# The output projection of a three-branch layer as seven block products instead of a plain tiled product

## The chip, the cores and the metric

The kernel runs on one core of one Trainium2 chip, in one launch. The metric is device time in microseconds (us). Three runs of the kernel before took 2734.89, 2730.94 and 2734.28 us, a median of 2734.28 us.

## The reference

Two layers are applied to x, a 1024 x 1024 matrix of fp32 (1024 positions, width 1024). Each layer norms x, multiplies it by w_in, runs three branches (an attention with top-k selection, a stick-breaking attention, an mLSTM), and mixes them; after both layers a last rms norm gives the output. What matters here is the end of a layer:

```
proj  = einsum('bsgc,gcd->bsgd', branches, w_branch)   # per branch 1024x512 by 512x1024
gates = sigmoid(merge)                                  # 3 x 1024 x 1024
mixed = sum over g of gates * proj                      # 1024 x 1024
x     = x + mixed @ w_out                               # 1024x1024 by 1024x1024
```

The next layer (or the end) begins with rms_norm of the rows of x.

## The kernel before

All products are done in float32r with a split: each operand is cut into a rounded part (hi, made by a ScalarE copy) and the remainder (lo, a subtraction on VectorE, or on GpSimd in pieces of 256 columns), and three passes hi·hi, hi·lo, lo·hi are summed in PSUM (`PASSES`). So each 128-deep step of a product is three matmuls.

The program is first written down as a log of operations by `body`; then the class `Plan` puts them in order. It walks through modelled time, gives each engine the ready operation that stands earliest in the log (`key`), gives each tile a buffer when its first operation is dispatched, and emits the whole in that order. Each engine then runs its own list strictly in that order. Tiles of SBUF are of two main sizes: `half` (128 x 520, `N_HALF` = 21 buffers) and `slab` (128 x 1032, `N_SLAB` = 35 buffers); a slab can also be split into two halves of the same type. `LOOK` (line 93) keeps an operation that needs a new half or slab from being taken more than 400 log entries ahead of the first one that is not done, and `room` (line 316) keeps an early tile from taking space that the log needs before it. PSUM has eight banks of 128 x 512: six of class `ps` and two of class `psf`. All DMAs are issued by the SP queue, in the plan's order.

The end of a layer (from line 1578): the gates were computed earlier and stored to DRAM (`gate_d`). For branches 2 and 1 (loop at line 1612) `load_y` brings the branch's hi and lo tiles, and for each of eight column blocks d and two row halves th `gate_proj` loads the gate and does 12 matmuls of 512 columns; VectorE multiplies, GpSimd adds into `mixed[d][th]`. For branch 0 the loop over th is outside: for each half of the rows, 8 x 12 matmuls, then VectorE adds and the sum is cut into hi and lo; then the output projection of this half: for each pair of column blocks cp two `load_w` of w_out (each 8 k-tiles: two DMAs of 512 KB, two ScalarE copies, eight GpSimd subtractions), and for four row tiles t two groups of 24 matmuls of 256 columns, after which VectorE adds the PSUM tile to the x row. So w_out and branch 0's weights are loaded and cut twice in a layer. Then the four rows are stored (`x_nd`, layer 0 only), normed in place (`norm_rows`: ScalarE square with sum, a small VectorE op, a power on GpSimd, a VectorE multiply `scalar_tensor_tensor` that writes the row back over itself), and `transpose_h` turns them with 32 TensorE transposes for the next layer; in the last layer the normed rows go to the output.

Of the kernel before, what the change touches and what calls it, by code (L numbers as in the profile page):

```python
# [11 lines left out]
F32R = mybir.dt.float32r  # L12
# [3 lines left out]
ALU = mybir.AluOpType  # L16
# [4 lines left out]
T = 1024  # L21
D = 1024
NB = 8
DEPTH = 2
# [9 lines left out]
PASSES = ((0, 0), (0, 1), (1, 0))  # L34
# [579 lines left out]
def body(log, tiles, caps, x_in, w_in, w_uk, w_uv, kvn, conv_w, ib, fb, mln, w_br, w_out, nrm, fnrm,  # L614
         rope_t, out, stop=None, dbg=None):
    V, S, G, PE, SY = (Engine(log, e) for e in ("DVE", "ACT", "POOL", "PE", "SP"))
# [6 lines left out]
    def slab(dt=F32):  # L623
        return tiles.new("slab", [128, 1032], dt)

    def half(dt=F32, n=520):
        return tiles.new("half", [128, n], dt)

    def pair(dt=F32):
        t = slab(dt)  # L630
        return t[:, 0:512], t[:, 512:1024]
# [8 lines left out]
    def pst(tag, n=512):  # L640
        return tiles.new(tag if tag == "psf" else "ps", [128, 512], F32)

    def dram(shape, dt=F32):
        return tiles.new("dram", shape, dt)
# [27 lines left out]
    for j in range(8):  # L672
        k = (j % 4) + 8 * (j // 4)
# [18 lines left out]
    def pool_tt(dst, a, b, op, n, w=256):  # L692
        for c in range(0, n, w):
            e = min(n, c + w)
            G.tensor_tensor(dst[:, c:e], a[:, c:e], b[:, c:e], op)

    def split(src, hi, lo, n=None):
        S.copy(hi, src)
        if n:
            pool_tt(lo, src, f(hi), ALU.subtract, n)  # L700
        else:
            V.tensor_tensor(lo, src, f(hi), ALU.subtract)

    def load_w(pieces, nk=8):
        W = [[], []]
        n = max(o + a.shape[1] for a, o in pieces)
        for hb in range(nk // 4):
            def view(t):
                return t[:, :1024].rearrange("p (k c) -> p k c", k=4)[:, :, :n]
            st, wh, wl = slab(), slab(F32R), slab(F32R)  # L710
            for a, o in pieces:
                m = a.shape[1]
                SY.dma_start(view(st)[:, :, o:o + m],
                             a[hb * 512:(hb + 1) * 512, :].rearrange("(k p) c -> p k c", p=128))
            S.copy(view(wh), view(st))
            for k in range(4):
                G.tensor_tensor(view(wl)[:, k], view(st)[:, k], f(view(wh)[:, k]), ALU.subtract)
            W[0].append(wh)
            W[1].append(wl)
        return W  # L720
# [13 lines left out]
    def acc_tc(p, W, n, sta, nk=8):  # L734
        i = 0
        for a, b in PASSES:
            for k in range(nk):
                PE.matmul(p[:, :n], sta(b, k), wcol(W, a, k, 0, n), start=(i == 0), stop=(i == 3 * nk - 1))
                i += 1
# [8 lines left out]
    def norm_rows(x, nw, dst):  # L748
        ss = small([128, 4], name="ss", bufs=8)
        junk = half(BF16, 1040)  # L750
        S.activation(junk[:, :1024], x[:, :1024], AF.Square, accum_out=ss[:, 0:1])
        V.tensor_scalar(ss[:, 1:2], ss[:, 0:1], 1.0 / D, EPS, ALU.mult, ALU.add)
        rsqrt(ss[:, 2:3], ss[:, 1:2])
        V.scalar_tensor_tensor(dst[:, :1024], x[:, :1024], ss[:, 2:3], nw[:, :1024], ALU.mult, ALU.mult)

    def transpose_h(hn, hT, th):
        for kb in range(8):
            p = pst("tr")
            for t in range(4):
                PE.transpose(p[:, t * 128:t * 128 + 128], hn[t][:, kb * 128:kb * 128 + 128], ident)  # L760
            hi, lo = pair(F32R)
            split(p, hi, lo)
            hT[0][kb][th], hT[1][kb][th] = hi, lo

    def new_hT():
        return [[[None, None] for _ in range(8)] for _ in range(2)]

    def load_row(vec):
        w = slab()
        SY.dma_start(w[:, :1024], bcast(vec, 1024))  # L770
        return w
# [9 lines left out]
    for th in range(2):  # L781
        hn = []
        for t in range(4):
            tb = th * 4 + t
            x = slab()
# [10 lines left out]
    x_res = x_in[0]  # L796
    for l in range(DEPTH):
# [25 lines left out]
        for tb in range(2, 8):  # L823
            if tb % 2 == 0:
                iq.append(half())
            p = pst("mm")
# [3 lines left out]
        for tb in range(8):  # L830
            if tb % 2 == 0:
                pb.append(half())
            p = pst("mm")
# [35 lines left out]
        for th in range(2):  # L869
            p = pst("tr")  # L870
# [7 lines left out]
        for tb in range(2, 8):  # L878
# [5 lines left out]
            p = pst("tr")  # L884
# [697 lines left out]
        def load_y(g, ths):  # L1582
            for b in range(4):
                for a in range(2):
                    if len(ths) == 2 and b < 2:
                        t = slab(F32R)
                        ym[b, a] = (t[:, 0:512], t[:, 512:1024])
                    else:
                        ym[b, a] = [half(F32R)[:, :512] if th in ths else None for th in range(2)]
                    for th in ths:  # L1590
                        SY.dma_start(f(ym[b, a][th]), f(y_d[g][a][b][:, th * 512:th * 512 + 512]))
# [4 lines left out]
        def gate_proj(Wm, Wp, j, th, kept=None):  # L1596
            g = half()
            if kept is None:
                p = pst("mm")
                acc_ct(p, Wm, j, mov, th)  # L1600
                S.activation(g[:, :512], p, AF.Sigmoid)
            else:
                SY.dma_start(g[:, :512], kept)
            p = pst("lg")
            acc_ct(p, Wp, j, ymov, th, nk=4)
            return g, p

        def wm(g, ct):
            return (None if g in AHEAD else load_w([(cols(C_MERGE + g * 1024 + ct * 256, 256), 0)]),
                    load_w([(w_br[l, g][:, ct * 256:ct * 256 + 256], 0)], nk=4))  # L1610

        for gi, g in enumerate((2, 1)):
            load_y(g, (0, 1))
            for ct in range(4):
                Wm, Wp = wm(g, ct)
                for j in range(2):
                    for th in range(2):
                        d = 2 * ct + j
                        gt_, p = gate_proj(Wm, Wp, j, th, gate_d.get((g, d, th)))
                        if gi == 0:  # L1620
                            mixed[d][th] = gt_
                            V.tensor_tensor(gt_[:, :512], gt_[:, :512], p, ALU.mult)
                        else:
                            V.tensor_tensor(gt_[:, :512], gt_[:, :512], p, ALU.mult)
                            pool_tt(mixed[d][th], mixed[d][th], gt_, ALU.add, 512)
        last = l == DEPTH - 1
        hT_n = new_hT()
        x_nd = None if last else dram([T, D])
        nwn = load_row(fnrm if last else nrm[l + 1])
        for th in range(2):  # L1630
            load_y(0, (th,))
            mx = [[None] * 8, [None] * 8]
            for ct in range(4):
                Wm, Wp = wm(0, ct)
                for j in range(2):
                    d = 2 * ct + j
                    gt_, p = gate_proj(Wm, Wp, j, th, gate_d.get((0, d, th)))
                    m = mixed[d][th]
                    V.tensor_tensor(gt_[:, :512], gt_[:, :512], p, ALU.mult)
                    V.tensor_tensor(m[:, :512], m[:, :512], gt_[:, :512], ALU.add)  # L1640
                    mx[0][d], mx[1][d] = hi, lo = pair(F32R)
                    split(m[:, :512], hi, lo)
            xs = []
            for cp in range(2):
                Wo = [load_w([(w_out[l][:, (2 * cp + i) * 256:(2 * cp + i) * 256 + 256], 0)]) for i in range(2)]
                for t in range(4):
                    tb = th * 4 + t
                    if cp == 0:
                        x = slab()
                        SY.dma_start(x[:, :1024], x_res[tb * 128:tb * 128 + 128, :])  # L1650
                        xs.append(x)
                    p = pst("mm")
                    for i in range(2):
                        acc_tc(p[:, 256 * i:256 * i + 256], Wo[i], 256,
                               lambda b, k: mx[b][k][:, t * 128:t * 128 + 128])
                    xx = xs[t][:, cp * 512:cp * 512 + 512]
                    V.tensor_tensor(xx, p, xx, ALU.add)
            hn = []
            for t in range(4):
                tb = th * 4 + t  # L1660
                if not last:
                    SY.dma_start(x_nd[tb * 128:tb * 128 + 128, :], xs[t][:, :1024])
                norm_rows(xs[t], nwn, xs[t])
                hn.append(xs[t])
                if last:
                    SY.dma_start(out[0, tb * 128:tb * 128 + 128, :], xs[t][:, :1024])
            if not last:
                transpose_h(hn, hT_n, th)
        hT = hT_n
        x_res = x_nd  # L1670
        if stop == "l0":
# [33 lines left out]
```

## Time and profile before

| | us |
|---|---|
| median of 3 runs | 2734.28 |
| the profiled execution | 2734.7 |
| its span, first to last instruction | 2732.9 |
| TensorE matmul busy | 2690.6 (98%) |
| VectorE busy | 1670.8 (61%) |
| ScalarE busy | 1474.7 (54%) |
| GpSimd busy | 1109.0 (41%) |
| mean granted TensorE clock | 0.996 of full speed |

Busy time is the time in which an engine had an instruction under way. PE is TensorE, PEld its weight loads (beside the matmuls), DVE is VectorE, ACT ScalarE, POOL GpSimd, SP the queue that issues DMAs. Since nearly every operation is emitted by one helper line (533), lines don't tell operations apart: shapes, engines and moments do. In layer 0 the end of the layer runs from about 1097 to 1382 us, in layer 1 from about 2500 us to the end.

### The profile page before, as it was taken

The numbers are of one execution on the slowest core, as the hardware profiler recorded it, in microseconds if no ns is written. First come the engines' busy times: TensorE is split into PE (matmuls) and PEld (weight loads), VectorE is DVE, ScalarE is ACT, GpSimd is POOL, SyncE is SP. The second block draws the span as 40 slices with busy tenths as digits, with TensorE's granted clock in tenths as the row PEclk, the third lists the DMA queues.
The fourth block names the chain that finished last, engine by engine and source line by source line (L and its number), as shares of the span: only waits on it lengthen the run. The fifth ranks groups of instructions, "written<-read, shape, count | busy, mean of one in ns | idle before, by whom it ended". The sixth has DMA issues, their size and how long they took to land.

```text
span 2732.9 us, 43639 instructions
## 1 busy us (share of the span) xinstructions
PE 2690.6 (98%) x15658; PEld 2306.7 (84%) x15666; DVE 1670.8 (61%) x3964; ACT 1474.7 (54%) x2961; POOL 1109.0 (41%) x1481
## 2 busy tenths in 40 slices
PE   8999999999999999999899999999999999999998
PEld 7888878888888888889898888888888888888898
DVE  5828788666686663424447287896676776624244
ACT  4637763545567766512236277735555577764131
POOL 4323333334253433455433233442342444334654
PEclk9999999999999999999999999999999999999999
DMA  4302112112132215745313022122121322246462
GB/s 131 97 16 80 37 57 83 39 55 82 31 103 61 78 54 177 243 143 206 104 41 109 24 62 62 51 67 66 39 74 33 102 64 77 61 167 231 161 206 77
DMA packets 251149, 249.53 MB, mean 91 GB/s; under 512 B 22378, under 2 KB 201908, under 8 KB 250932
## 3 DMA queue, kind: packets, MB, share of 16 engines
q1 hardware_dynamic: 250932, 246.75, 28.5%
q8 instruction: 123, 2.02, 0.3%
q14 instruction: 94, 0.77, 0.1%
HBM read 184.37 MB, written 62.32 MB: 90 GB/s over the span
## 4 chain that ended last, share of the span: by engine, by line
PE 52%; ACT 3%; DVE 2%; issue 1%; DMA 1%; POOL 1%; SPq 0%; POOLq 0%; DVEq 0%; ACTq 0%
PE t L533 52%; ACT t L533 2%; DVE t L533 1%; POOL t L533 1%; ACT s L533 1%; DMA d<-t 0%; DMA t<-in_w_in_dram 0%; ACT L533 0%; DVE s L533 0%; SPq L533 0%; DMA t<-d 0%; POOLq L1701 0%; DVEq L533 0%; ACTq L533 0%; POOLq L533 0%
## 5 line engine op out<-in xcount | busy, mean ns | idle before, releaser
L533 PE MATMUL t<-t,t 128*128 128x512 f32 (+5 forms) x15466 | 2669.2, 336 | 34.7 <-DVE t L533 29.2
L533 PEld LDWEIGHTS t<-t,t 128*128 128x128 f32 x15330 | 2271.0, 184 | 394.9 <-DVE t L533 41.2
L533 POOL TENSOR_TENSOR t<-t,t 128x256 fp32r<-128x256 f32 (+4 forms) x1092 | 875.7, 830 | 1178.8 <-ACT t L533 470.9
L533 DVE TENSOR_TENSOR t<-t,t 128x512 f32<-128x512 f32 (+14 forms) x1514 | 757.4, 532 | 691.0 <-ACT t L533 498.3
L533 ACT CAST t<-t 128x512 fp32r<-128x512 f32 (+6 forms) x1073 | 563.9, 569 | 520.3 <-PE t L533 238.7
L533 ACT ACTIVATE t<-t 128x512 f32<-128x512 f32 (+4 forms) x704 | 350.8, 593 | 339.6 <-PE t L533 216.3
L533 ACT ACTIVATE t<-t,t 128x768 bf16<-128x768 f32 (+10 forms) x352 | 279.1, 813 | 26.4 <-DVE t L533 18.3
L533 ACT COPY t<-t 64x256 f32<-64x256 f32 (+4 forms) x294 | 109.4, 377 | 267.1 <-PE t L533 262.9
L533 DVE TENSOR_TENSOR_SCAN t<-t 128x256 f32<-128x256 f32 (+10 forms) x144 | 210.5, 1473 | 6.5 <-ACT t L533 6.2
L533 DVE SCALAR_TENSOR_TENSOR t<-t,t,t 128x512 f32<-128x512 f32 (+8 forms) x214 | 162.3, 777 | 28.4 <-DMA d<-t 11.6
L533 POOL TENSOR_SCALAR t<-t 64x512 fp32r<-64x512 f32 x128 | 85.1, 666 | 194.2 <-ACT t L533 157.7
L533 ACT ACT_TABLE_LOAD x111 | 142.4, 1283 | 25.9 <-PE t L533 13.4
L533 POOL TENSOR_SCALAR t<-t,t 128x256 f32<-128x256 f32 (+7 forms) x128 | 95.4, 754 | 138.4 <-DVE t L533 126.1
L533 DVE TENSOR_SCALAR_CACHE_REDUCE t<-t,t 128x512 bf16<-128x512 f32 (+2 forms) x173 | 128.3, 768 | 0.9
L533 DVE TENSOR_TENSOR s<-s,t 128x512 f32<-128x512 f32 x70 | 51.5, 737 | 96.3 <-PE t L533 96.2
L533 DVE CUSTOM_DVE_ANT_0 t<-t,t 128x512 f32<-128x512 f32 (+3 forms) x160 | 92.6, 591 | 20.9 <-PE t L533 17.6
L533 DVE TENSOR_SCALAR t<-t 128x1 f32<-128x1 f32 (+5 forms) x324 | 59.1, 188 | 24.0 <-ACT t L533 21.6
L533 PE MATMUL t<-s,t 128*128 128x512 f32 (+1 forms) x192 | 62.3, 379 | 0.0
L533 DVE RECIPROCAL t<-t 128x1 f32<-128x1 f32 (+1 forms) x144 | 23.0, 163 | 56.1 <-ACT t L533 55.2
L533 DVE TENSOR_TENSOR t<-t 128x1 f32<-128x1 f32 (+9 forms) x234 | 53.0, 238 | 4.7 <-POOL t L533 2.3
L533 ACT ACTIVATION_READ_ACCUMULATOR t<-t,t 128x1 f32 x280 | 52.9, 189 | 0.0
L533 ACT ACTIVATE s<-t,t 128x896 bf16<-128x896 f32 (+2 forms) x40 | 41.6, 1041 | 15.0 <-DVE s L533 14.5
(37 smaller groups left out, 417.4 us busy)
## 6 DMA issues: line engine op xcount, KB each, us to landing
t<-in_w_in_dram SPq DMA_DIRECT2D x192, 256.0 KB
d<-t SPq DMA_DIRECT2D x134, 256.0 KB
t<-d SPq DMA_DIRECT2D x128, 256.0 KB
t<-in_w_in_dram SPq DMA_DIRECT2D x44, 512.0 KB
s<-d SPq DMA_DIRECT2D x76, 256.0 KB
d<-t SPq DMA_DIRECT2D x130, 128.0 KB
t<-in_w_branch_dram SPq DMA_DIRECT2D x32, 512.0 KB
t<-in_w_out_dram SPq DMA_DIRECT2D x32, 512.0 KB
```

What stands on the lines that cost most here:

```text
L533: fn(*args, **kw)
```

## The change

The loop over branches becomes `(2, 1, 0)`: branch 0 is projected for both row halves together, its weights are loaded once, VectorE adds its part to `mixed`. The output projection becomes Strassen's scheme in Winograd's form: mixed and w_out are taken as 2 x 2 blocks of 512 x 512; eight sums of blocks (four of mixed, four of w_out, four tiles of 128 x 512 each, all on VectorE) and seven block products. Each operand of a product is cut into hi and lo just before it (`cut`: the left one with VectorE, the right one with GpSimd). A product is four row tiles of 12 matmuls of 512 columns; the partial sums stay in PSUM (X over four products, Y over two, Z for one) and after each row tile VectorE adds the PSUM tile as it then stands to the right quarter of x. w_out comes once, as 16 tiles of 256 KB; the x rows of both halves are loaded ahead. In layer 0 the normed rows go to tiles of their own (`h = slab()`) instead of over x.

```
-        for gi, g in enumerate((2, 1)):
+        for gi, g in enumerate((2, 1, 0)):
             load_y(g, (0, 1))
...
+        def cut(xs_, pool):
+            hs, ls = [], []
+            for x in xs_:
+                hi, lo = half(F32R)[:, :512], half(F32R)[:, :512]
+                split(x, hi, lo, 512 if pool else None)
...
+        def prod(ps_, A, B, first, th, c):
+            for t in range(4):
+                i = 0
+                for a, b in PASSES:
+                    for k in range(4):
+                        PE.matmul(ps_[t], A[b][k][:, t * 128:t * 128 + 128], B[a][k],
+                                  start=first and i == 0, stop=i == 11, skip_group_check=True)
+                        i += 1
+                x = xs[4 * th + t][:, c * 512:c * 512 + 512]
+                V.tensor_tensor(x, ps_[t], x, ALU.add)
...
+                    SY.dma_start(x_nd[tb * 128:tb * 128 + 128, :], xs[tb][:, :1024])
+                    h = slab()
+                    norm_rows(xs[tb], nwn, h)
...
+        A1, B1 = cut(mA[0][0], False), cut(wo[0][0], True)
+        X = [pst("mm") for _ in range(4)]
+        prod(X, A1, B1, True, 0, 0)
+        T1 = sums(wo[0][1], wo[0][0], ALU.subtract, V)
+        T2 = sums(wo[1][1], T1, ALU.subtract, V)
+        A2, B2 = cut(mA[0][1], False), cut(wo[1][0], True)
+        Z = [pst("psf") for _ in range(4)]
+        prod(Z, A2, B2, True, 0, 0)
+        S1 = sums(mA[1][0], mA[1][1], ALU.add, V)
+        S2 = sums(S1, mA[0][0], ALU.subtract, V)
+        A6, B6 = cut(S2, False), cut(T2, True)
+        prod(X, A6, B6, False, 1, 0)
+        A5, B5 = cut(S1, False), cut(T1, True)
+        prod(X, A5, B5, False, 1, 1)
+        S4 = sums(mA[0][1], S2, ALU.subtract, V)
+        A3, B3 = cut(S4, False), cut(wo[1][1], True)
+        prod(X, A3, B3, False, 0, 1)
+        S3 = sums(mA[0][0], mA[1][0], ALU.subtract, V)
+        T3 = sums(wo[1][1], wo[0][1], ALU.subtract, V)
+        A7, B7 = cut(S3, False), cut(T3, True)
+        Y = [pst("psf") if t < 2 else pst("mm") for t in range(4)]
+        prod(Y, A7, B7, True, 1, 1)
+        nwn = load_row(fnrm if last else nrm[l + 1])
+        T4 = sums(wo[1][0], T2, ALU.subtract, V)
+        A4, B4 = cut(mA[1][1], False), cut(T4, True)
+        finish_x(0)
+        prod(Y, A4, B4, False, 1, 0)
+        finish_x(1)
```

## Rows read from the trace of the kernel before

**Rows 1.** The page's first part: busy us, share and count of each engine.

```profile
PE 2690.6 (98%) x15658; PEld 2306.7 (84%) x15666; DVE 1670.8 (61%) x3964; ACT 1474.7 (54%) x2961; POOL 1109.0 (41%) x1481
```

**Rows 2.** Waits of PE: who waited for whom, us in all, times, longest.

```profile
PE t L533 <- DVE t L533: 29.2, 18, 7.9
PE t L533 <- ACT t L533: 1.4, 3, 0.8
PE t L533 <- POOL t L533: 1.3, 3, 1.0
PE t L533 <- DMA t<-d: 0.5, 1, 0.5
```

**Rows 3.** Timeline, middle of layer 0's end: start, length, engine, operation, idle before it.

```profile
1300.04 0.33 SPq L533 DMA_DIRECT2D d<-t  x1
...
1300.46 1.01 SPq L533 DMA_DIRECT2D t<-in_x_dram  x2
...
1306.96 1.65 DVE L533 SCALAR_TENSOR_TENSOR t<-t,t,t 128x1024 f32<-128x1024 f32 x1 [5.52 <-DMA d<-t]
...
1308.67 1.97 PE L533 MATMUL t<-t,t 128*128 128x128 f32 x7 [7.41 <-DVE t L533]
```

**Rows 4.** Windows of PE around it: length, PE busy, granted clock, DMA share, GB/s.

```profile
1306.00:1308.60 2.60, 0.00 (x0) 0.50 0.68 274
1308.60:1310.00 1.40, 1.33 (x7) 0.50 0.01 6
...
1311.00:1312.00 1.00, 1.00 (x7) 0.50 0.00 0
1312.00:1313.00 1.00, 1.00 (x7) 0.64 0.00 0
1313.00:1314.00 1.00, 1.00 (x7) 1.00 0.00 0
```

**Rows 5.** Windows of PE: 96 matmuls of 512 columns, and 384 of 256.

```profile
1152.26:1174.45 22.19, 22.19 (x97) 1.00 0.79 280
2679.80:2725.30 45.50, 45.49 (x385) 1.00 0.08 31
```

**Rows 6.** Timelines of DVE and POOL where the other engine was idle.

```profile
2606.34 0.69 DVE L533 TENSOR_TENSOR t<-s,t 128x512 fp32r<-128x512 f32 x1
2606.95 0.68 DVE L533 TENSOR_TENSOR s<-s,t 128x512 f32<-128x512 f32 x1
2607.67 0.69 DVE L533 TENSOR_TENSOR s<-s,s 128x512 f32<-128x512 f32 x1
```
```profile
2631.29 5.67 POOL L533 TENSOR_TENSOR t<-t,t 128x256 fp32r<-128x256 f32 x8 [12.07 <-issue]
```

**Rows 7.** Groups by shape, 2664.2 to 2679.7 us, DVE and POOL both busy throughout.

```profile
L533 DVE TENSOR_TENSOR s<-s,t 128x512 f32<-128x512 f32 x5 | 5.6, 1137 | 0.0
L533 DVE TENSOR_TENSOR t<-t,t 128x512 f32<-128x512 f32 x7 | 5.2, 755 | 0.1
L533 DVE TENSOR_TENSOR t<-s,t 128x512 fp32r<-128x512 f32 x3 | 3.1, 1045 | 0.0
L533 DVE TENSOR_TENSOR t<-t,t 128x512 fp32r<-128x512 f32 x2 | 2.5, 1230 | 0.0
L533 DVE SCALAR_TENSOR_TENSOR t<-t,t,t 128x1024 f32<-128x1024 f32 x1 | 1.8, 1764 | 0.4 <-POOL t L533 0.4
```
```profile
L533 POOL TENSOR_TENSOR t<-t,t 128x256 fp32r<-128x256 f32 x16 | 17.2, 1113 | 0.0
```

**Rows 8.** Timeline of ACT: eight casts of 512 columns in a row.

```profile
1388.86 4.04 ACT L533 CAST t<-t 128x512 fp32r<-128x512 f32 x8
```

**Rows 9.** Windows of all engines, the branch loops of layers 0 and 1.

```profile
1145.00:1212.00 67.00, 67.00 (x304) 54.92 (x303) 18.28 (x28) 11.00 (x14) 28.13 (x40) 1.00 0.63 217
2500.00:2590.00 90.00, 90.00 (x414) 73.70 (x413) 26.59 (x43) 16.26 (x23) 46.97 (x67) 1.00 0.54 189
```

**Rows 10.** Timeline of the end: the last row after the last matmul.

```profile
2725.32 0.69 DVE L533 TENSOR_TENSOR t<-t,t 128x512 f32<-128x512 f32 x1 [1.64 <-PE t L533]
2726.05 1.06 ACT L533 ACTIVATE t<-t 128x1024 bf16<-128x1024 f32 x1 [4.50 <-DVE t L533]
...
2728.05 1.28 DVE L533 SCALAR_TENSOR_TENSOR t<-t,t,t 128x1024 f32<-128x1024 f32 x1 [0.66 <-POOL t L533]
2729.36 0.33 SPq L533 DMA_DIRECT2D out_dram<-t  x1
```

More of the change, by code (lines that the diff above doesn't have):

```diff
@@ L1610, in wm @@
                     load_w([(w_br[l, g][:, ct * 256:ct * 256 + 256], 0)], nk=4))
-        for gi, g in enumerate((2, 1)):
+        last = l == DEPTH - 1
+        hT_n = new_hT()
+        x_nd = None if last else dram([T, D])
+        for gi, g in enumerate((2, 1, 0)):
             load_y(g, (0, 1))
@@ L1619, in body @@
                         gt_, p = gate_proj(Wm, Wp, j, th, gate_d.get((g, d, th)))
+                        V.tensor_tensor(gt_[:, :512], gt_[:, :512], p, ALU.mult)
                         if gi == 0:
                             mixed[d][th] = gt_
-                            V.tensor_tensor(gt_[:, :512], gt_[:, :512], p, ALU.mult)
-                        else:
-                            V.tensor_tensor(gt_[:, :512], gt_[:, :512], p, ALU.mult)
-                            pool_tt(mixed[d][th], mixed[d][th], gt_, ALU.add, 512)
@@ L1626, in body @@
[L1626 to L1657, printed above, removed]
@@ new lines, in body, with sums @@
+                        elif gi == 1:
+                            pool_tt(mixed[d][th], mixed[d][th], gt_, ALU.add, 512)
+                        else:
+                            V.tensor_tensor(mixed[d][th][:, :512], mixed[d][th][:, :512], gt_[:, :512], ALU.add)
+        def sums(a, b, op, eng):
+            r = []
+            for x, y in zip(a, b):
+                t = half()[:, :512]
+                if eng is G:
+                    pool_tt(t, x, y, op, 512)
+                else:
+                    eng.tensor_tensor(t, x, y, op)
+                r.append(t)
+            return r
@@ new lines, in cut @@
+        def cut(xs_, pool):
[3 more added lines that the diff above has]
+                split(x, hi, lo, 512 if pool else None)
+                hs.append(hi)
+                ls.append(lo)
+            return hs, ls
+        wo = [[[], []], [[], []]]
+        for j, c in ((0, 0), (1, 0), (0, 1), (1, 1)):
+            for k in range(4):
+                t = half()[:, :512]
+                SY.dma_start(t, w_out[l][(4 * j + k) * 128:(4 * j + k) * 128 + 128, c * 512:c * 512 + 512])
+                wo[j][c].append(t)
@@ new lines, in body @@
+        mA = [[[mixed[4 * j + k][th][:, :512] for k in range(4)] for j in range(2)] for th in range(2)]
+        xs = []
+        for tb in range(8):
+            x = slab()
+            SY.dma_start(x[:, :1024], x_res[tb * 128:tb * 128 + 128, :])
+            xs.append(x)
+        def prod(ps_, A, B, first, th, c):
+            for t in range(4):
+                i = 0
+                for a, b in PASSES:
+                    for k in range(4):
+                        PE.matmul(ps_[t], A[b][k][:, t * 128:t * 128 + 128], B[a][k],
[3 more added lines that the diff above has]
+                V.tensor_tensor(x, ps_[t], x, ALU.add)
@@ L1658, in body, with finish_x @@
+        def finish_x(th):
             hn = []
@@ L1660, in body @@
                 tb = th * 4 + t
[L1661 to L1664, printed above, removed]
                 if last:
-                    SY.dma_start(out[0, tb * 128:tb * 128 + 128, :], xs[t][:, :1024])
+                    norm_rows(xs[tb], nwn, xs[tb])
+                    SY.dma_start(out[0, tb * 128:tb * 128 + 128, :], xs[tb][:, :1024])
+                else:
+                    SY.dma_start(x_nd[tb * 128:tb * 128 + 128, :], xs[tb][:, :1024])
+                    h = slab()
+                    norm_rows(xs[tb], nwn, h)
+                    hn.append(h)
             if not last:
                 transpose_h(hn, hT_n, th)
+        A1, B1 = cut(mA[0][0], False), cut(wo[0][0], True)
[26 more added lines that the diff above has]
+        finish_x(1)
         hT = hT_n
```

## The prediction

> **What bounds the kernel now.** I read four views, in this order. The page's first part shows matmuls under way for 2690.6 of 2732.9 us [rows 1]; the next engine has 61%. A busy matmul engine alone proves little, so the second view is the list of PE's waits: 32.4 us in all [rows 2]. PE is a bound by its own list: what is taken out of that list comes off the time, as long as the other engines deliver in time. The third view, the timeline, shows the longest wait outside the start: 7.41 us in the middle of layer 0's end, where PE stands before the first transposes of the normed rows [rows 3]. These wait for the row's last multiply on DVE, and that waits for a DMA that stores the same row to DRAM, since it writes over it; the store was issued at 1300.04 and let go at 1306.96, with loads of x issued behind it. The fourth, windows, shows what the gap costs beyond itself: the granted clock is at 0.50 (1.2 instead of 2.4 GHz) at the end of the gap and until about 1312.7 [rows 4].
>
> **Term 1, the matmuls.** Before, a layer's output projection is 8 row tiles x 4 column blocks x 24 = 768 matmuls of 256 columns. 384 of them filled 45.5 us without a hole [rows 5], 118.5 ns each: 91.0 us a layer. After, it is 7 products x 4 row tiles x 12 = 336 matmuls of 512 columns; 96 of these took 22.19 us [rows 5], 231.1 ns each: 77.7 us. The difference is 13.3 us a layer, 26.7 us in all (product: 12.3 from the eighth multiplication saved, the rest because one wide matmul takes less than two narrow ones). Branch 0 keeps its 192 matmuls a layer.
>
> **Term 2, the gap.** With tiles of their own the normed rows no longer wait for the store. 7.41 us of wait go, and the 4.0 us at half clock behind it held 2.0 us of work more at full clock [rows 3, 4]: 9.4 us. What is late next: the same row's chain on ACT, DVE, POOL and DVE, 4.0 us from its last add to the end of its multiply when nothing is in the way (2725.32 to 2729.33) [rows 10], and POOL, which has a queue of cuts. But now PE has the seventh and the fourth product to do beside it, and the transposes stand in PE's list where the planner thinks them ready. Bounds of what comes back: 0 to 9.4; I charge 1 us, near the low end, since no DMA is in that chain any more.
>
> **Term 3, the work added beside PE.** For each product DVE makes four lo tiles and four adds from PSUM, POOL eight subtractions of 256 columns, ACT eight casts; and there are 32 tiles of sums a layer, all on DVE. Per layer DVE has 28 + 28 + 32 = 88 operations on 128 x 512, POOL 56. Against that go DVE's 16 cuts and 16 adds and POOL's 64 subtractions of the old projection, and half of the 32 for branch 0's weights. ACT has 56 casts at 0.505 us [rows 8], 28 us in 77.7: no bound. DVE and POOL get in each other's way. Alone, a DVE operation takes 0.69 us and POOL's 0.71 [rows 6]; with both busy those DVE operations that read two SBUF tiles take 1.05 to 1.23 and POOL's 1.11, while most reading PSUM stay near 0.69 [rows 7].
>
> Is the stage bound by that? Before the last product starts, 66.6 us after the first, DVE must have done 24 adds and 56 operations on SBUF tiles, POOL 48. By 0.69 us alone that is 55.2 us for DVE. If each of the 48 POOL operations held DVE up by the contended excess (1.13 mean of the ten slow ones less 0.69, 0.44), 21.1 us more: 76.3. The 24 adds take 16.6 us in which POOL can do 23 of its 48 freely, so some 25 collide: 55.2 + 25 x 0.44 = 66.2 us, level with PE's 66.6. The best row is the window itself [rows 7]: in 15.5 us DVE did 17 such operations and one twice as long while POOL did 16, which scales to 13.6 and 11.5 in a product's 11.1 us; the new stage wants 13.3 and 8. So it fits, with DVE near full and little to spare, and the two products that need two block sums each before their cut (sixth and seventh: 12 operations on SBUF tiles and 4 adds) a little over. Each layer can lose from 0 (PE has no wait there that could go) to 18.2 us here (18.2 if no POOL operation ran beside an add: 56 x 0.61 + 48 x 0.71 + 24 x 0.69 = 84.8 less 66.6, with 0.61 the distance of two starts on DVE [rows 6]). I take 2.5 a layer, near the window's rate.
>
> The Trainium skill has a rule that speaks against this change: by "SBUF — State Buffer", section "SBUF: two separate sides", a VectorE operation with two SBUF inputs and a GpSimd operation that reads SBUF exclude each other, and the loser blocks for the whole instruction. The rows agree with exclusion in kind; in size they are milder, since a colliding pair would cost 0.61 + 0.71 = 1.32 us by it and took 1.11 to 1.13 [rows 6, 7]. By that rule the stage would lose at least 1.6 us a layer (56 x 0.61 + 48 x 0.71 = 68.2 against 66.6), more where the adds give no cover.
>
> **Term 4, buffers.** Halves and slabs make 21 + 2 x 35 = 91 half tiles. Counting by the log: while the first product runs, 64 are held (16 mixed, 16 of w_out, 16 for x, 16 cuts); second 68; sixth 76; fifth 68; third 60; seventh 44. To cut for the next product while one runs wants 16 to 24 more, while w_out's first block goes free: 84, 92, 92, 88, 84, 64. So the cuts of the next product fit, short by one tile at two places of six, where the last tile is made late. This is in the 2.5 us a layer; below zero it can't go.
>
> **Term 5, transfers.** w_out falls from 8 to 4 MB a layer, branch 0's weights from 4 to 2 MB; DMAs issued for them from 24 to 20 a layer. Branch 0's y tiles must now come for both halves at once and the x rows before the first product, behind branch loops that already use DMA to 0.54 to 0.63 [rows 9]. PE had no wait for these loads there, so there is nothing to gain, and branches 2 and 1 load as much per matmul. I cost it at 0; if the cover is gone, P1's adds wait, not PE.
>
> **Term 6, the end.** From the last matmul to the last instruction's end are 7.6 us (2725.3 to 2732.9) [rows 10]. The chain stays; rows now finish every 2.77 us (12 x 231.1 ns) instead of 5.6, so a row's 1.28 us multiply can sit in front of the next add. 0 to 1.3 us; I take 0.6.
>
> **Sum**, against the profiled execution's 2734.7 us (span 2732.9; the median of the runs shown is 0.4 lower): 26.7 + 9.4 - 1 - 5 - 0 - 0.6 = 29.5 us less, **2705 us**. Elsewhere the planner's order may shift from layer 1 on; PE's waits there and in the rest of the kernel are a few us, either way, and I add 3 to both sides.
>
> **Rivals.**
> (a) *The stage is bound by DVE with POOL.* Its full price, 18.2 us a layer: 2734.7 - 26.7 - 9.4 + 1.6 + 36.4 = 2736.6, no change. Half of it: 2718. For it: DVE near 100% by my own count, and its order is fixed, so one late add holds the next cut. Against: the window of rows 7, and ACT and POOL have room. By the exclusion rule named above its least price, 3.2 us, lies inside my forecast.
> (b) *The gap comes back.* Transposes in PE's list ahead of the fourth product, rows not ready: 9.4 us with its slow clock, 2734.7 - 26.7 + 5 + 0.6 = 2713.6. For it: that is how the gap of before arose. Against: the store is out of the chain.
> (c) *Buffers don't let the next product's cut run ahead; slower.* Place: each of the six borders between products. If a cut starts only when the product before is done, the first product row waits for five casts (2.5 us) and eight POOL subtractions (5.7) less the 2.8 us that the row itself lasts: 5.4 us, and 2 us of half clock as behind the gap of before: 7.4 us a border, twelve borders. Five blocked borders cost more than the 36.1 us that terms 1 and 2 give; with seven 2734.7 - 36.1 + 51.8 = 2750. For it: 92 wanted of 91 at two borders, and halves of different type can't share a slab. Against: four borders have 3 halves or more free, and the planner places what it can, not all or nothing.
> (d) *The saving is not on the path.* PE has no other holes that could take up 26.7 us [rows 2], so I give it nothing of its own; it is inside (a).
>
> **Chances.** Forecast 0.64, its own range 2697 to 2714; (a) 0.16, spread evenly from 2714 to 2737; (b) 0.09; (c) 0.11. Lowest plausible: nothing lost in terms 2, 3 and 6 and 3 us gained elsewhere, 2695.6. For 8 in 10 I leave out (c) and the upper half of (a): 2695 to 2724. What can be told from no change is 0.2%, 5.5 us (2728.8 to 2739.8): (a)'s uppermost third is the same, 0.06; slower is (c), 0.11; faster the rest, 0.83.
>
> **What would show it.** In the profile after: 672 wide matmuls in the place of 1536 narrow ones, so PE busy near 2664 us; no DVE multiply that waits for a store in the middle; clock 1.00 throughout the end of layer 0; seven blocks of 11.1 us in each layer with holes of 1 us or less before them, DVE busy above 80% in the stage. It is wrong if those blocks stand apart by 3 us and more (a, c: (a) with DVE full before the hole, (c) with DVE idle and waiting for PE), or if a hole with low clock stands before the transposes (b).

## The result, and the profile after

The changed kernel takes 2701.32 us (median of 4 runs, 2700.3 to 2702.44) against 2734.22 (4 runs of the kernel before, 2730.94 to 2734.89): ratio 0.9884, 95% interval 0.9872 to 0.9896. That is 32.9 us less where 29.5 were forecast; 2705 was 3.7 us too high, inside the likeliest case's own range of 2697 to 2714. The profiled execution took 2701.0 us, its span is 2699.2, against 2734.7 and 2732.9 before.

The first part of its page, the line of busy times (engine, us, share of the span, instructions):

```profile
PE 2660.6 (99%) x14802; PEld 2245.6 (83%) x14802; DVE 1753.4 (65%) x4076; ACT 1484.8 (55%) x3004; POOL 1086.3 (40%) x1433
```

PE works 30.0 us less than in [rows 1] and stands idle 38.6 us instead of 42.3. DVE has 83 us more to do, and PE waits less for it than in [rows 2]. The list of PE's waits after (who waited for whom, us in all, times, longest):

```profile
PE t L533 <- DVE t L533: 22.2, 20, 7.9
PE t L533 <- ACT t L533: 1.9, 6, 0.4
PE t L533 <- POOL t L533: 1.0, 4, 0.5
```

Layer 1's seven products in windows of 11.1 us, one for each (length; busy us and count of PE, PEld, DVE, ACT, POOL; granted clock; DMA share; GB/s):

```profile
2610.60:2621.70 11.10, 11.10 (x49) 8.95 (x48) 7.34 (x11) 2.81 (x6) 5.45 (x6) 1.00 0.45 180
2621.70:2632.80 11.10, 11.10 (x50) 8.99 (x49) 6.98 (x10) 4.26 (x9) 2.34 (x4) 1.00 0.14 47
2632.80:2643.90 11.10, 11.10 (x50) 8.96 (x49) 7.29 (x10) 4.62 (x10) 7.04 (x8) 1.00 0.00 0
2643.90:2655.00 11.10, 11.10 (x50) 9.01 (x49) 10.78 (x14) 3.52 (x7) 10.47 (x11) 1.00 0.01 1
2655.00:2666.10 11.10, 11.10 (x50) 8.97 (x48) 9.13 (x13) 7.40 (x13) 7.76 (x10) 1.00 0.00 1
2666.10:2677.30 11.20, 11.20 (x49) 8.87 (x48) 10.09 (x14) 3.65 (x6) 6.72 (x9) 1.00 0.00 0
2677.30:2688.40 11.10, 11.10 (x49) 8.71 (x47) 8.48 (x14) 2.19 (x5) 6.29 (x7) 1.00 0.48 191
sum 77.80, PE 77.80 PEld 62.46 DVE 60.09 ACT 28.44 POOL 46.07; mean PE 11.11 PEld 8.92 DVE 8.58 ACT 4.06 POOL 6.58
```

Seven products, 77.80 us, PE busy for all of it: the forecast's 77.7 without a hole. DVE is full only in the fourth window (10.78 of 11.10) and has 77% on the whole, a little under the 80% that the prediction named. Layer 0's end is tighter, because the norms, the transposes and the next layer's loads lie in it; the window over the middle of it (same columns):

```profile
1300.00:1360.00 60.00, 60.00 (x291) 49.35 (x289) 54.53 (x73) 28.61 (x50) 53.41 (x57) 1.00 0.33 111
```

PE has no idle time and the clock stays at 1.00, with DVE at 91% and POOL at 89%. This is the stretch that held the hole of [rows 3] and the half clock of [rows 4]. What stands there now is seen in the timeline (start, length, engine, operation):

```profile
1341.87 4.88 DVE L533 SCALAR_TENSOR_TENSOR t<-t,t,t 128x1024 f32<-128x1024 f32 x3
...
1343.15 0.60 PE L533 MATMUL t<-t,t 128*128 128x128 f32 x4
...
1345.22 1.07 PE L533 MATMUL t<-t,t 128*128 128x128 f32 x6
```

The rows' multiplies wait for nothing, and the transposes (128 columns) go in handfuls between the last product's wide matmuls.

**Where the 33.7 us of span went.** All from the two traces:

```
matmuls: 2 x (768 x 118.5 ns - 336 x 231.5 ns)          -26.4
the hole in the middle of layer 0's end                  -7.4
half clock while PE works: 13.7 us before, 3.3 after     -5.2
the end, from the last matmul: 7.62 to 10.79             +3.2
PE's other holes                                         +0.5
not placed                                               +1.6
```

While PE works, a stretch at half clock costs half its length: behind the hole of the kernel before, wide matmuls start 0.427 us apart at 0.50 (1310.4 to 1311.3) and 0.231 us at 1.00 (1314 to 1316). Of the 5.2 us, 2.0 belong to the hole that is gone (Term 2 had them); 1.7 to a hole of 2.25 us in layer 1 (from 1715.6) that is gone too, though nothing of the change was meant for it; 1.5 lie at a place that the change doesn't touch, as the windows of the kernel before show here:

```profile
347.00:350.50 3.50, 3.18 (x11) 2.80 (x12) 3.47 (x10) 2.79 (x7) 1.42 (x2) 0.50 0.00 0
350.50:353.60 3.10, 3.10 (x13) 2.67 (x13) 0.14 (x2) 1.83 (x5) 2.84 (x4) 0.50 0.00 0
...
1715.00:1718.00 3.00, 0.75 (x6) 0.44 (x5) 1.69 (x4) 2.95 (x8) 0.00 (x0) 1.00 0.00 0
...
1718.90:1722.30 3.40, 3.40 (x13) 2.67 (x12) 2.19 (x8) 1.69 (x6) 2.53 (x4) 0.50 0.00 0
```

and the same place of the changed kernel:

```profile
347.00:350.50 3.50, 3.27 (x12) 2.90 (x12) 3.46 (x10) 2.69 (x7) 1.51 (x3) 0.51 0.00 0
350.50:353.60 3.10, 3.10 (x22) 2.69 (x21) 1.24 (x3) 2.41 (x7) 2.77 (x4) 1.00 0.00 0
```

In both a hole of 3.8 to 3.95 us ends at about 347 us, in layer 0, long before the output projection. Before, the clock was low until 353.6 and PE did 13 matmuls in the second 3.1 us; after, it was back at 350.5 and PE did 22. The last section compares this place in all fourteen traces.

**The end** is 3.2 us longer. Timeline of the changed kernel's last 20 us, its main lines:

```profile
2680.70 4.87 DVE L533 SCALAR_TENSOR_TENSOR t<-t,t,t 128x1024 f32<-128x1024 f32 x4 [1.59 <-POOL t L533]
...
2685.49 1.88 DVE L533 TENSOR_TENSOR t<-t,t 128x512 f32<-128x512 f32 x3
...
2687.80 0.63 PE L533 MATMUL t<-t,s 128*128 128x512 f32 x2
...
2688.47 0.69 DVE L533 TENSOR_TENSOR t<-t,t 128x512 f32<-128x512 f32 x1 [1.10 <-PE t L533]
...
2689.35 1.04 ACT L533 ACTIVATE t<-t 128x1024 bf16<-128x1024 f32 x1
...
2691.20 4.51 SPq L533 DMA_DIRECT2D out_dram<-t  x4
...
2692.86 2.48 DVE L533 SCALAR_TENSOR_TENSOR t<-t,t,t 128x1024 f32<-128x1024 f32 x2 [0.38 <-POOL t L533]
```

Four multiplies of the first half hold DVE from 2680.70 to 2685.57, and the last product's first adds stand behind them. So the four last rows come to the norm together. Their squares run on ACT without a gap, the last from 2689.35, 0.88 us after the start of the last add (0.73 before); then the rows stand in each other's way on POOL and DVE, and the last two multiplies run back to back from 2692.86 to 2695.34. Before, the last row found every engine free, and its multiply ended 4.0 us after the start of its last add [rows 10]; now 6.9 us pass.

### The profile page after: what moved, and what is told of

Same layout as the page of the kernel before. It is cut to its first block, busy times and chain, and to the rows that moved or that the text cites. A ratio compares the mean times of both kernels' runs of the same rounds, so it can differ in the third digit from the quotient of the medians.

```text
span 2699.2 us, 42025 instructions
## 1 busy us (share of the span) xinstructions
PE 2660.6 (99%) x14802; PEld 2245.6 (83%) x14802; DVE 1753.4 (65%) x4076; ACT 1484.8 (55%) x3004; POOL 1086.3 (40%) x1433
## 4 chain that ended last, share of the span: by engine, by line
PE 51%; ACT 4%; DVE 2%; issue 1%; DMA 1%; POOL 0%; SPq 0%; DVEq 0%; ACTq 0%; POOLq 0%
PE t L533 51%; ACT t L533 3%; DVE t L533 2%; ACT s L533 1%; DMA t<-in_w_in_dram 1%; ACT L533 1%; POOL t L533 0%; DVE s L533 0%; SPq L533 0%; DMA d<-t 0%; DVEq L1751 0%; ACTq L533 0%; DVEq L533 0%; POOLq L533 0%
## 5 line engine op out<-in xcount | busy, mean ns | idle before, releaser
L533 PE MATMUL t<-t,t 128*128 128x512 f32 (+5 forms) x14094 | 2536.7, 342 | 27.8 <-DVE t L533 22.2
L533 PEld LDWEIGHTS t<-t,t 128*128 128x128 f32 x13950 | 2114.0, 183 | 397.6 <-DVE t L533 36.2
L533 POOL TENSOR_TENSOR t<-t,t 128x256 fp32r<-128x256 f32 (+3 forms) x946 | 754.3, 825 | 1074.3 <-ACT t L533 446.0
L533 DVE TENSOR_TENSOR t<-t,t 128x512 f32<-128x512 f32 (+15 forms) x1514 | 761.6, 534 | 592.7 <-ACT t L533 489.0
L533 ACT ACTIVATE t<-t 128x512 f32<-128x512 f32 (+5 forms) x699 | 346.9, 592 | 266.4 <-PE t L533 196.5
L533 ACT ACTIVATE t<-t,t 128x768 bf16<-128x768 f32 (+7 forms) x343 | 273.6, 817 | 25.7 <-DVE t L533 19.6
L533 DVE SCALAR_TENSOR_TENSOR t<-t,t,t 128x512 f32<-128x512 f32 (+7 forms) x220 | 166.7, 781 | 12.5 <-POOL t L533 5.3
L533 DVE TENSOR_TENSOR s<-s,t 128x512 f32<-128x512 f32 (+1 forms) x93 | 67.4, 728 | 106.4 <-PE t L533 103.7
L533 DVE TENSOR_SCALAR_CACHE_REDUCE t<-t,t 128x512 bf16<-128x512 f32 (+5 forms) x169 | 125.7, 770 | 1.0
L533 PE MATMUL t<-t,s 128*128 128x512 f32 (+1 forms) x200 | 63.3, 389 | 0.0
```

The source lines that it names most:

```text
L533: fn(*args, **kw)
```

## The experiments

The times are medians; each ratio is to runs of the kernel before on the same chip beside them.

**e1_own_tiles: the old projection, with own tiles for the normed rows.** One edit in the kernel before:

```diff
-                norm_rows(xs[t], nwn, xs[t])
-                hn.append(xs[t])
+                h = xs[t] if last else slab()
+                norm_rows(xs[t], nwn, h)
+                hn.append(h)
```

> The kernel before with one edit: in layer 0 the normed rows go to tiles of their own. My theory (term 2): the 7.41 us wait for the store and 2.0 us lost at half clock go, 9.4 us less, ratio about 0.9966 (2725 us), and no DVE multiply in the middle of layer 0's end waits for a store. Rival (b): the transposes still stand in PE's list before the rows are ready, since ACT, DVE and POOL are as slow as before; then the hole shrinks to some 3 to 5 us and the gain is 2 to 5 us.

Measured: 2731.01 us (11 runs), ratio 0.9993 (0.9984 to 1.0002). The timeline around the hole:

```profile
1297.26 13.52 POOL L533 TENSOR_TENSOR t<-t,t 128x256 fp32r<-128x256 f32 x17 [0.23 <-ACT t L533]
...
1303.62 1.74 DVE L533 SCALAR_TENSOR_TENSOR t<-t,t,t 128x1024 f32<-128x1024 f32 x1 [1.55 <-POOL t L533]
...
1305.41 6.75 PE L533 MATMUL t<-t,t 128*128 128x128 f32 x28 [3.48 <-DVE t L533]
```

The wait for the store is gone, as said; the hole is 3.48 us instead of 7.41, and the clock is at 0.50 for 3.4 us instead of 6.8, with PE at work for 3.4 instead of 4.1 of them. What is late next is the row's own chain, through POOL, where 17 cuts of 256 columns stand in one block. Own tiles alone gain nothing that is clear of the noise, and at most 4.4 us (the interval's lower end), not 9.4; the profiled execution, 2728.5 us, is among the shortest of the eleven. The rival named a hole of 3 to 5 us, as came, and a gain of 2 to 5; the medians give 1.7.

**e2_seven_inplace: the other half.** The changed kernel, with the norm written over its row again:

```diff
-                    h = slab()
+                    h = xs[tb]
                     norm_rows(xs[tb], nwn, h)
```

> The changed kernel, but the normed rows are written over the rows as before. My theory: with the fourth product (11 us) logged behind the transposes' inputs, PE has matmuls to do while the store lands, so the wait for the store costs PE 0 to 3 us: 2701 to 2704 us. Rival: the hole of before returns whole with its slow clock, 9.4 us more: about 2711 us. The first would mean that the own tiles are not what removed the hole here, the second that they are.

Measured: 2700.71 us, ratio 0.9882 (0.9869 to 0.9896): no worse than the changed kernel's 2701.32, and no hole. SP's timeline, the first and the last of the four stores of the first half's rows:

```profile
1325.36 0.34 SPq L533 DMA_DIRECT2D d<-t  x1
...
1333.96 0.34 SPq L533 DMA_DIRECT2D d<-t  x1
```

and the timeline where these rows are multiplied and transposed:

```profile
1342.19 1.28 DVE L533 SCALAR_TENSOR_TENSOR t<-t,t,t 128x1024 f32<-128x1024 f32 x1
...
1344.75 4.80 DVE L533 SCALAR_TENSOR_TENSOR t<-t,t,t 128x1024 f32<-128x1024 f32 x3
...
1346.03 0.60 PE L533 MATMUL t<-t,t 128*128 128x128 f32 x4
```

The last store is issued 8.2 us before the first of these multiplies, where [rows 3] had 6.9 us from the issue to the release, and PE has block products to do all the while: its transposes begin at 1346.03, 12.1 us behind the last store. So the own tiles are not what removed the hole.

**e3_eight_products: the same blocks without the saved product.** Each quarter of the result is 4 row tiles x 24 matmuls of 512 columns, each block cut once, one add for each tile:

```diff
-        A1, B1 = cut(mA[0][0], False), cut(wo[0][0], True)
...
+        def prod8(A, B, th, c):
...
+        P0, Q0 = cut2(mA[0], False), cut2([wo[0][0], wo[1][0]], True)
+        prod8(P0, Q0, 0, 0)
+        Q1 = cut2([wo[0][1], wo[1][1]], True)
+        prod8(P0, Q1, 0, 1)
+        P1 = cut2(mA[1], False)
+        prod8(P1, Q0, 1, 0)
         finish_x(0)
-        prod(Y, A4, B4, False, 1, 0)
+        prod8(P1, Q1, 1, 1)
```

> The changed kernel with the plain eight block products of 512 columns instead of seven: no block sums, each block cut once, rest as in the changed kernel. My theory (term 1): PE-bound, 384 wide matmuls a layer instead of 336, 48 x 231.5 ns = 11.1 us a layer more: 22.2 us, 2723.5 us, within 4. Rival (a): the sums and the cuts beside seven products cost PE something hidden, and without them part of the 22 us is given back: 2712 us or less.

Measured: 2721.85 us, ratio 0.996 (0.9948 to 0.9972), 20.5 us over the changed kernel. In the window over its last products (columns as above) DVE has 18.76 us of work in 72:

```profile
2640.00:2712.00 72.00, 71.97 (x311) 57.98 (x309) 18.76 (x27) 8.06 (x14) 3.87 (x7) 1.00 0.12 48
```

Two layers of 48 matmuls at 231.1 ns are 22.2 us. In the two spans, 2720.1 and 2699.2, this one has an end of 8.10 us instead of 10.79 (2.7 less) and works for 5.2 us at half clock at 347 us instead of 3.3 (1.0 more): 22.2 - 2.7 + 1.0 = 20.5, measured 20.9. Against the kernel before it gains 10.9 us in the medians and 12.8 between the two profiled spans. Of the 12.8, 7.4 are the hole, which it does not have either, 4.5 come from wide instead of narrow matmuls (2 x (91.0 - 384 x 0.2311)) and 4.3 from less half clock; 0.5 at the end, 1.1 in other holes and 1.8 not placed go against it.

**g1_merged_loop: the kernel before, with branch 0 in the same loop as the others.** Its weights are loaded once in a layer:

```diff
-        for gi, g in enumerate((2, 1)):
+        for gi, g in enumerate((2, 1, 0)):
...
-            load_y(0, (th,))
...
+            for d in range(8):
+                mx[0][d], mx[1][d] = hi, lo = pair(F32R)
+                split(mixed[d][th][:, :512], hi, lo)
```

> The kernel before with branch 0 projected for both row halves in one loop (its weights loaded once); the old output projection of 256 columns, its weights loaded twice, and the norm in place. My theory (term 5): loading once is worth nothing by itself, PE's list is as long; and the hole of 7.4 us stays, since nothing but the old projection of the second half is left to run beside the first half's norm: 2730 to 2736 us. Rival: the hole came from how the planner placed the transposes between branch 0's second half and the projection; with the loop merged it goes with its 2 us of slow clock, 2722 to 2726 us, and then it is the loop, not the seven products nor the own tiles, that removed it.

Measured: 2733.35 us (11 runs), ratio 1.0004 (0.9995 to 1.0013): nothing. The hole stays, in the same form:

```profile
1323.67 0.33 SPq L533 DMA_DIRECT2D d<-t  x1
...
1329.92 1.45 DVE L533 SCALAR_TENSOR_TENSOR t<-t,t,t 128x1024 f32<-128x1024 f32 x1 [4.91 <-DMA d<-t]
...
1331.42 3.84 PE L533 MATMUL t<-t,t 128*128 128x128 f32 x17 [6.93 <-DVE t L533]
```

Half the traffic for branch 0's weights is not what counts, nor is the moved branch (w_out is still loaded twice here). Together with e2 and e3 that leaves the new projection, with seven or eight products, as what keeps the hole away. Want of other work is not why PE stood in the kernel before: behind the transposes its list held the second half's branch 0 (8 x 12 wide matmuls), as the group by shape in the window from 1313.2 to 1335.6 us of its trace shows (count with one that overlaps the window's edge, busy us, mean ns, idle before):

```profile
L533 PE MATMUL t<-t,t 128*128 128x512 f32 x97 | 22.8, 395 | 0.0
```

What differs is where the transposes stand in that list. Before, PE came at 1301.26 (1308.67 less 7.41) to those that need the first half's last row, 1.2 us after that row's store was issued at 1300.04 [rows 3]. In e2 a whole product lies between the rows' last adds and the log's place for their norm, and PE comes to the first transposes 12.1 us after the last store; in e3 it is 21 us (1321.63 to 1342.98). That this place alone decides is argued from these times: no run gave the old projection a later place, or the seven products an earlier one in layer 0.

**f1_dve_plus1 and f2_dve_plus3: how near is DVE to its limit?** Every lo tile of the mixed operand (28 a layer) is computed twice, or four times; nothing of the computation is left out.

```diff
                 split(x, hi, lo, 512 if pool else None)
+                if not pool:
+                    for _ in range(1):      # f2: range(3)
+                        V.tensor_tensor(lo, x, f(hi), ALU.subtract)
```

> The changed kernel with each of the 28 subtractions of a layer that cut a left operand done twice in a row on VectorE (56 operations of 128 x 512 more in all, same result). In the changed kernel DVE is busy for 60.1 of the 77.8 us of layer 1's seven products and for 72.1 of 82.0 in layer 0's, and PE has no hole there. My theory (term 3, DVE near its edge): 28 x 0.69 to 1.13 us, 19 to 32 us, no longer fit beside PE in either layer; the time rises by 5 to 25 us, with holes of PE that DVE ends. Rival: DVE has that much room, since a waiting DVE operation is counted as busy; the time stays within 2 us of 2701.

> The same with each of these subtractions done four times (168 operations more in all). My theory: DVE needs at least 60 + 84 x 0.69 = 118 us for 77.8 us of products: 35 to 45 us a layer more, 2770 to 2790 us. Under the rival too it must be slower by 25 us or more a layer; if it is not, DVE is no bound of this stage at all.

Measured: f1 2722.84 us, ratio 0.996 (0.9947 to 0.9972); f2 2803.49, ratio 1.0253 (1.0237 to 1.0269). With 56 operations more the loss is 21.5 us, 0.38 each; with 168 it is 102.2, 0.61 each, above the 70 to 90 that I expected. f1's windows over the ends of layers 0 and 1:

```profile
1274.00:1370.00 96.00, 89.97 (x379) 69.74 (x378) 88.41 (x112) 34.83 (x62) 67.55 (x66) 0.96 0.24 76
2622.00:2709.00 87.00, 82.03 (x346) 63.75 (x344) 80.65 (x106) 27.16 (x49) 53.99 (x51) 1.00 0.10 39
```

and its PE timeline, three of the holes:

```profile
1341.48 7.41 PE L533 MATMUL t<-t,t 128*128 128x512 f32 x24 [2.22 <-DVE t L533]
...
1357.35 1.72 PE L533 MATMUL t<-t,t 128*128 128x512 f32 x5 [2.21 <-DVE t L533]
...
2690.92 1.65 PE L533 MATMUL t<-t,t 128*128 128x512 f32 x6 [2.21 <-DVE t L533]
```

DVE is now busy 92 to 93% and PE waits for it, 30.3 us in the list of waits instead of 22.2; f2's list has

```profile
PE t L533 <- DVE t L533: 73.5, 41, 8.0
```

Layer 1's stage had 17.7 us of DVE idle (77.8 less 60.1); 28 operations of the 0.61 us that they take alone [rows 6] would be 17.1 and just fit. They don't, since beside POOL such an operation took 0.92 us on the mean in this window (0.89 to 1.08 by group). The holes are short, but three of them are followed by 3.4 us at half clock. Of the 21.8 us between the spans of f1 and the changed kernel, 12.2 are holes, 5.0 half clock and 1.9 the end; 2.7 are not placed. Rival (a) is real, at most 28 operations a layer away.

**f3_early_cut, e4_early_both, f4_early_mid: the end.** In the order of the log the seventh product (A7, B7) is the sixth and the fourth (A4, B4) the last. In f3 the last product's operands are made before the seventh product instead of after it; e4 and f4 also give the first half's norm, in the last layer, an earlier place in the log: e4 behind the third product, f4 between the seventh's cut and the fourth's sums.

```diff
+        nwn = load_row(fnrm if last else nrm[l + 1])
+        T4 = sums(wo[1][0], T2, ALU.subtract, V)
+        A4, B4 = cut(mA[1][1], False), cut(T4, True)
         Y = [pst("psf") if t < 2 else pst("mm") for t in range(4)]
         prod(Y, A7, B7, True, 1, 1)
-        nwn = load_row(fnrm if last else nrm[l + 1])
-        T4 = sums(wo[1][0], T2, ALU.subtract, V)
-        A4, B4 = cut(mA[1][1], False), cut(T4, True)
         finish_x(0)
```

```diff
         prod(X, A3, B3, False, 0, 1)
+        nwn = load_row(fnrm if last else nrm[l + 1])
+        if last:
+            finish_x(0)      # e4; in f4 behind the cut of A7, B7
...
```

> The changed kernel with only the last product's sums and cuts logged ahead of the seventh product's matmuls; the norm of the first half stays where it is. My theory: the last product's rows no longer run interleaved for want of lo tiles, its first two rows end some 2 us earlier, and DVE's four multiplies of the first half end earlier as well: the end falls from 10.8 us by 1 to 2 us, 2699 to 2700 us, without the hole of 4.5 us that the kernel with both moves has before its seventh product. Rival: the sums ahead of the seventh product delay that product, a hole of 1 to 4 us with slow clock, 2702 to 2708 us.

> The changed kernel with two moves in the log: the operands of the last product are summed and cut ahead of the seventh product's matmuls, and in the last layer the norm of the first four rows is logged right behind the product that finishes them. In the changed kernel 10.8 us pass from the last matmul to the end, against 7.6 before, since four norms of the first half stand on DVE in front of the last product's adds. My theory: the end falls to 7.6 to 8.5 us and the time by 2 to 3 us, to 2698 to 2699 us. Rival: the order in DVE's list just moves the delay into PE, holes of 1 to 3 us before the seventh or the last product, and the time stays at 2701 or rises.

> As the one before, and in the last layer the norm of the first four rows is logged behind the seventh product's cuts and ahead of the last product's. My theory: the seventh product's operands come first, so no hole there; the four multiplies are done before the last product's adds, the end falls to 8 us, 2698 to 2699 us. Rival: the last product's cuts come late instead, a hole of 2 to 5 us with slow clock before it, 2704 to 2708 us.

Measured: f3 2705.06 us, ratio 0.9896 (0.9882 to 0.9909); e4 2709.95, 0.9916 (0.9902 to 0.9929); f4 2711.77, 0.992 (0.9907 to 0.9934). e4 and f4 are slower than the change; f3's interval overlaps its own, though each of its four runs is longer than each of the changed kernel's. None gains the 1 to 3 us that I expected. The end becomes 9.92, 8.02 and 8.17 us long instead of 10.79: with the first half's multiplies out of the way it is within 0.6 us of the kernel before's 7.6. Of the 2.6 to 2.8 us, early operands alone (f3) give 0.9 and the earlier multiplies the rest. But a new hole stands in e4 before the seventh product and in f4, 6.46 us, before the last. e4's PE timeline there:

```profile
2678.37 1.94 PE L533 MATMUL t<-t,t 128*128 128x512 f32 x5 [4.51 <-DVE t L533]
```

and its DVE timeline just before:

```profile
2674.20 2.96 DVE L533 SCALAR_TENSOR_TENSOR t<-t,t,t 128x1024 f32<-128x1024 f32 x2 [0.44 <-POOL t L533]
```

DVE does the multiplies while PE waits for its cuts; 3.4 us at half clock follow in e4, and 10.2 in f4, of which PE works 6.0. Besides, each of the three has holes of 2.2 and 1.9 to 2.1 us at about 1693 and 2102 us, far from the edit, and all but f4's second are followed by 3.4 us at half clock; the changed kernel has none over 0.7 us at the first place and 1.25 us at the second. The planner's order moved; why it moved at those places I did not find out.

**g2_pool_t3, g3_pool_t1t3, g4_pool_t3_early: sums moved from DVE to POOL.** g2 moves T3, g3 T1 as well, g4 is g2 with f3's edit:

```diff
         T2 = sums(wo[1][1], T1, ALU.subtract, V)
+        T3 = sums(wo[1][1], wo[0][1], ALU.subtract, G)
...
-        T3 = sums(wo[1][1], wo[0][1], ALU.subtract, V)
```

> The changed kernel with one of the eight block sums of a layer (the difference of w_out's right blocks, four tiles, eight operations) moved from VectorE to GpSimd and logged early, where GpSimd has idle time. The doubled subtractions showed 0.38 us of time for each DVE operation put in; my theory is that taking some out gives only the end of the last layer, since PE has no other hole: 0.5 to 2 us less, 2699 to 2701 us. Rival: GpSimd's eight operations collide with DVE's and with its own cuts, and the time stays or rises by up to 3 us.

> The same with two block sums on GpSimd. My theory: as before, the end alone can gain, at most the 3.2 us by which it grew: 2698 to 2701 us. Rival: the second sum is needed for the second product's successor early, GpSimd makes it late, and holes cost 2 to 6 us.

> One block sum on GpSimd, and the last product's operands logged ahead of the seventh product's matmuls. Early operands alone gave an end of 9.9 us instead of 10.8 but 2705 us, with a hole of 2.2 us and its slow clock in the middle of layer 1, far from the edit, as the planner's order shifted. My theory: 2698 to 2701 us if that hole does not come, since the end shortens; rival: such holes come and go with any edit of the log, 2702 to 2707 us.

Measured: 2704.16 us (0.9896, 0.988 to 0.9911), 2704.08 (0.9895, 0.9882 to 0.9909) and 2702.66 (0.989, 0.9876 to 0.9903). The ends shrink to 9.50, 8.67 and 9.52 us, and holes of 1.63 (g2, at 2279), 0.98 and less (g3, inside the stage) and 2.13 us (g4, at 2098) take it back. None beats the changed kernel; the intervals of g2 to g4 overlap its own. The traces of g2 and g4 are those of their shortest executions, with spans 0.7 and 1.0 us over the changed kernel's, so they don't show why the medians are 2.8 and 1.3 us over it.

## Why the prediction was right, step by step

**Term 1 (26.7) was right in sum.** PE's busy time fell by 30.0 us: 26.4 in the matmuls, at 231.5 ns for each wide one, and 5.2 at half clock, less the 1.6 not placed. e3 shows the eighth product alone (20.9 of span against 20.5 worked out with its other differences). The 4.5 us of wide instead of narrow matmuls are read from the rates of the two traces; no run has them alone. The split in brackets was wrong: 48 matmuls of 231.1 ns are 11.1 us a layer, not 12.3, and the wide matmuls give 2.3.

**Term 2 (9.4, less 1) had the right size and the wrong cause.** The hole and its slow clock are gone: 7.4 + 2.0. The step that failed is that "with tiles of their own" the whole 7.41 us of wait go: e1 has the tiles, no wait for the store and still a hole of 3.48 us, and e2 writes over the rows as before and has no hole. That 9.4 came out is luck as far as the tiles go; e1 gains 4.4 at most. What the runs leave is what I gave as a side reason, that PE has products to do beside the norm; more exactly, that the transposes stand in PE's list a product behind the rows that they need. That place is not shown apart from the products themselves. The charge of 1 us was not needed. Rival (b) did not come.

**Term 3 (5.0) was charged and not spent.** PE was busy for all of the 77.8 us, and in layer 0 for all of 82 from 1274 to 1356. The collisions are there; of the groups by shape in layer 1's stage (count, busy us, mean ns, idle before) the adds from PSUM kept their speed and POOL's subtractions did not:

```profile
L533 DVE TENSOR_TENSOR t<-t,t 128x512 f32<-128x512 f32 x28 | 19.3, 706 | 12.9 <-PE t L533 12.7
...
L533 POOL TENSOR_TENSOR t<-s,s 128x256 fp32r<-128x256 f32 x13 | 12.7, 1004 | 10.8 <-issue 8.8 <-PE t L533 1.5 <-DVE s L533 0.6
```

But DVE had idle time to pay with. My count made the stage a draw (66.2 against 66.6) by letting each of 25 POOL operations hold DVE up in full; it kept 23% idle in layer 1. The trace shows slowed pairs and no loss. By the rule of the Trainium skill ("SBUF — State Buffer", "SBUF: two separate sides") that the loser blocks for the whole instruction, the prediction's estimate was a loss of at least 1.6 us a layer; the trace does not agree with that size, since PE is busy for 77.80 of 77.80 us. f1 shows that the reserve is small: the charge was too high for this load and would be too low for one with 28 operations more.

**Term 4 (buffers) held**: PE has no hole at any of the twelve borders, so rival (c) fell. **Term 5 (0) held**: g1, with half the loads of branch 0's weights, is at 1.0004, and PE has no wait in the changed kernel from 1150 to 1365 us.

**Term 6 (0.6, at most 1.3) failed**: the end grew by 3.2 us. I counted one multiply in front of one add. There are four, because the first half's norm runs beside the last product, and they make the four last rows arrive together. The ends of e4 and f4, 8.02 and 8.17 us, show it against f3's 9.92: their edits differ from f3's in the place of the first half's norm alone. The other 0.9 us, which f3 gives, belong to the late cuts of the last product's operands.

The distance to the forecast, from the span: 5 and 1 us not spent in terms 3 and 2, 3.2 us less half clock that I had not counted, against 2.6 more at the end, 0.5 in other holes, 0.3 in the matmuls and 1.6 not placed: 4.2 us, 33.7 against 29.5. The total was nearer than its parts, since the errors have both signs; that is luck, and so are the 1.5 us of half clock at the place that the change doesn't touch.

## What to carry to other kernels

A wait that is named in the profile can be hidden by other work as well as removed, so "what is late next" is to be answered for both ways: here a log in which the waiting matmuls come a product later went with the end of a hole that the new tiles alone only halved. An engine's reserve is measured best by giving it more: 28 operations a layer that DVE could take by its idle time and its times alone cost 21.5 us. At the end of a kernel count everything that the last rows' chain meets on each engine, not one instruction of it.

## What the runs showed of the hardware

The clock fell behind holes much shorter than the 7.41 us of [rows 3]: behind 2.25 us in the kernel before (1715.6), behind 2.2 us in f1, f3, e4 and f4, and behind 1.93 us in e4 (2102.1) it was at 0.50 for 3.4 us; but not behind 2.17 us in g1 (1715.5), nor behind 2.21 us in f1 (2688.7), 2.13 us in g4 (2097.7) and 2.04 us in f4 (2102.8). The hole of 3.8 to 4.0 us that ends at about 347 us was followed by 6.8 us at half clock in the profiled executions of before, e1, g1 and e3, and by 3.4 us in those of the changed kernel and all its other variants, ten in all. The moment at which the clock fell sorts the two: in the four it fell 0.6 to 1.7 us before the hole ended, in the ten at most 0.25 us before its end, or after it. Between the two profiled executions of before and after that is 1.5 us of span, at a place where all kernels compute the same. Why the early falls come in these four, I do not know; a second trace of one kernel would tell, and there is none.
